# First sums of weight blocks: ScalarE and an adding DMA in place of a VectorE subtraction

## The chip, the cores and the metric

The kernel runs on one core of one Trainium2 chip. The metric is device time in microseconds (us) of one execution. The engines are named as the profile names them: PE (TensorE matmul), PEld (its weight load), DVE (VectorE), ACT (ScalarE), POOL (GpSimd), SP (SyncE, which issues the DMAs of the kernel before).

## What is computed

Two layers of a decoder over 512 tokens of 1024 features, all in float32. Layer 0 mixes tokens with gated linear attention (GLA), layer 1 with retention. Around each mixer stand two feed-forward blocks, so there are four of these; each ends in a layer norm.

```
def swiglu(x, w_in, w_out):
    gate, up = jnp.split(x @ w_in, 2, axis=-1)
    return (jax.nn.silu(gate) * up) @ w_out

def reference(x, ...):
    h = x
    for i in range(DEPTH):                      # DEPTH = 2
        h = layer_norm(DN_ALPHA * h + 0.5 * swiglu(h, ffn_w_in[i, 0], ffn_w_out[i, 0]), ...)
        m = gla_mixer(h, ...) if i == 0 else retention_mixer(h, ...)
        h = layer_norm(DN_ALPHA * h + m, ...)
        h = layer_norm(DN_ALPHA * h + 0.5 * swiglu(h, ffn_w_in[i, 1], ffn_w_out[i, 1]), ...)
    return h
```

`w_in` is 1024 x 5632 (gate and up of 2816 features), `w_out` 2816 x 1024.

## The kernel before

Weights come as granules of 1 MiB (128 partitions x 2048 float32), in the order in which they are used. `Stream` (lines 77 to 146) holds two load buffers `wf`: `load` (L92) has SP fetch granule i into one, and `prepare` (L108) makes from it the operands that PE takes. A float32 matrix product is done in three passes on operands that are split into hi + lo: `parts` (L101) casts a tile to hi on ACT (L105) and subtracts hi from it on DVE for lo (L106). `mm3` (L148) issues the three matmuls (L151 to L153). `next` (L137) returns granule i and prepares i + 1.

In a feed-forward block the hidden features come in 22 tiles of 128. For features 4 to 21 (`FAST`, 18 in each of the four blocks, 72 in all) gate and up are not taken as eight block products but as seven, `seven_products` (L323), by Winograd's form of Strassen's method over halves of tokens, input features and outputs. It needs sums of blocks of the weights, and these are what the change touches. With the granule's four blocks b11, b12, b22, b21 of 128 x 512, `prepare` forms the tile `t13` = [b12 - b11, b22 - b12] in one DVE subtraction over 1024 columns (L129), then `t24` = [b22 - t1, b21 - t2] in two over 512 (L130, L131), and splits both (`parts(st, t24)`, `parts(su, t13)`). Both tiles take the tag "sums", of which there are two buffers. The operands land in five buffers of 1024 columns and two of 512 (`slot`, L98), so a granule can be split only once PE is through with an earlier one.

The products of one such granule go to PSUM and are combined by DVE (L346, L348, L351, L353, L355) and ACT (L343, L349); the second product of a granule is written into the bank whose last content L351 reads. Between two such granules and the next two stands one granule of the output matrix (`out_steps`, L294), whose four results DVE adds to h (L275 or L277). So the order of use repeats itself: an odd feature X, an even feature Y, an output granule O, then X', Y', O'. A block has nine such pairs of X and Y, with the first pair partly at its start.

The order on each engine is not the order of the code: a scheduler of the framework sorts each engine's queue when the program is built, and puts semaphores where one engine reads what another wrote. Each queue is then worked through in order, so an instruction that waits holds up all behind it on its engine. POOL does nothing in the feed-forward blocks but L210, a power for the layer norm.

Names in the rows: `wf` a load buffer, `whi`/`wlo` the split weights, `sums` t13 or t24, `u`, `v`, `gate`, `up` and `products` those of `seven_products`, `sg`, `ahi`, `alo` the activation, `po` the output product.

Of the kernel before, what the change touches and what calls it, by code (L numbers as in the profile page):

```python
# [14 lines left out]
ALU = mybir.AluOpType  # L15
AX = mybir.AxisListType

P = 128
T = 512
NT = T // P  # L20
D = 1024
# [10 lines left out]
G = 2048  # L32
B = 512
GH, GDK, GDV, GRANK = 4, 128, 256, 16
RH, RDK, RDV = 4, 256, 512
CH = 64


def _ffn_plan():
    """The order of a feed-forward block's granules: ("in", f) for gate and up of  # L40
    128 features, ("out", c, i) for four units of the output product of chunk c,
    which lie between the features of the next chunk."""
    plan = []
    for c, (f0, f1) in enumerate(CHUNKS):
        n = 0
        for f in range(f0, f1):
            plan.append(("in", f))
            if c and (f - f0) % 2 == 0 and n < (CHUNKS[c - 1][1] - CHUNKS[c - 1][0]) // 2:
                plan.append(("out", c - 1, n))
                n += 1  # L50
    return plan + [("out", len(CHUNKS) - 1, i) for i in range((CHUNKS[-1][1] - CHUNKS[-1][0]) // 2)]


def _fast():
    """The granules of feed-forward weights that seven products take."""
    r, at = set(), 0
    plan = _ffn_plan()
    for mixer in (0, GH * 3 + GH, 0, RH * 6 + 2 * RH):
        at += mixer
        r |= {at + i for i, x in enumerate(plan) if x[0] == "in" and x[1] in FAST}  # L60
        at += len(plan)
    return r
# [3 lines left out]
def tile_decoder(ctx: ExitStack, tc: tile.TileContext, a: dict, out: bass.AP):  # L66
# [8 lines left out]

    # ---------------------------------------------------------------- weights
    class Stream:
        """The weights, 1 MiB at a time in the order of their use, each split
        exactly into two float32r parts."""

# [20 lines left out]
        def parts(self, slot, src, at=0):  # L101
            """src as hi + lo."""
            n = src.shape[-1]
            hi, lo = (x[:, at:at + n] for x in slot)
            nc.scalar.copy(hi, src)  # L105
            nc.vector.tensor_sub(lo, src, hi.bitcast(F32))  # L106

        def prepare(self, i):  # L108
# [3 lines left out]
            w = self.loaded[i]  # L112
            blk = lambda slot, c: tuple(x[:, c * B:(c + 1) * B] for x in slot)  # noqa: E731
            if i not in fast:
# [13 lines left out]
            t13, t24 = (self.sums_pool.tile([P, 2 * B], F32, tag="sums", name="sums", bufs=2) for _ in range(2))  # L128
            nc.vector.tensor_sub(t13, w[:, B:3 * B], w[:, :2 * B])  # L129
            nc.vector.tensor_sub(t24[:, :B], b22, t13[:, :B])  # L130
# [17 lines left out]
    def mm3(ps, l, r, start, stop):  # L148
        """One K tile of a float32 product: (hi + lo) x (hi + lo), with the three
        passes that reach float32's precision."""  # L150
        nc.tensor.matmul(ps, l[0], r[0], start=start, stop=False)  # L151
        nc.tensor.matmul(ps, l[0], r[1], start=False, stop=False)  # L152
        nc.tensor.matmul(ps, l[1], r[0], start=False, stop=stop)  # L153
# [3 lines left out]

    # ---------------------------------------------------------------- start
    hT = [None]
# [36 lines left out]

    # ---------------------------------------------------------------- layer norm
    def load_gb(tp, n, tags=("ln_g", "ln_b")):
# [7 lines left out]
    def rsqrt(tp, out_, in_, eps, n, scale=1.0):  # L206
        """(scale * (in_ + eps)) ** -0.5"""
        v = tp.tile([P, n], F32, tag="veps", name="veps", bufs=2)
        nc.vector.tensor_scalar(out=v, in0=in_, scalar1=eps, scalar2=scale, op0=ALU.add, op1=ALU.mult)
        nc.gpsimd.tensor_tensor(out=out_, in0=v, in1=mhalf[:, :n], op=ALU.pow)  # L210

    def layer_norm(tp, t, gb, last):
        """h[t] <- LN(h[t]); its transpose into hT."""
        x = h[t]
# [20 lines left out]

    # ---------------------------------------------------------------- products
    def feature_major(w, ranges, ps=None):
        """out[feature, token] of 2 tiles of 128 features."""
        w = [tuple(x.rearrange("p (k c) -> p k c", k=4) for x in b) for b in w]
        ps = ps or [pacc.tile([P, T], F32, tag="acc", name="fm") for _ in range(2)]  # L240
        for j in range(2):
            for r in ranges:
                for k in range(KD):
                    mm3(ps[j][:, r], pick(w[j if k < 4 else 3 - j], slice(None), k % 4),
                        pick(hT[0], slice(None), k, r), k == 0, k == KD - 1)
        return ps
# [6 lines left out]
    def two_granules_ahead():  # L253
        """The first two granules after a layer norm: the first half of the tokens
        is taken first, while the norm of the second half ends."""
        g = [ws.next(), ws.next()]
# [6 lines left out]
    def token_major(t, ws2, ps):  # L263
        """out[token, 512 columns] of one token tile."""
        for k in range(KD):
            mm3(ps, pick(hT[0], slice(None), k, slice(t * P, (t + 1) * P)), ws2[k // 4][k % 4], k == 0, k == KD - 1)
# [3 lines left out]
    def add_out(t, half, ps, first, tp=None):  # L270
        """h[t] <- alpha * h[t] + ps, or h[t] + ps; with tp, what the layer norm
        needs of it."""
        x = h[t][:, half * 512:(half + 1) * 512]
# [9 lines left out]
    class Units:  # L283
        """Units [P, 512] of the coming granules, four in each."""

# [8 lines left out]
    def out_steps(lhs, n, first, halves=(0, 1), tp=None):  # L294
        """h[:, half] += lhs^T @ W for all tokens, one K tile after the other: the
        steps, each to be given its unit."""
        for half in halves:
# [13 lines left out]
    def out_by_tokens(lhs, n, units, halves, first, tail=None, tp=None):  # L311
        """The same, one token tile after the other."""
        for t in range(NT):
# [7 lines left out]

    # ---------------------------------------------------------------- feed-forward
    def seven_products(w, s, tp):  # L323
        """gate and up [feature, token] of 128 features with the seven products of
        Winograd's form of Strassen's method, over halves of the tokens, of the
        features of h and of the outputs (gate and up)."""
        a11, a12, a22 = (pick(hT[0], slice(None), ks, ts)
# [12 lines left out]
        x, y, z, q = (bank(*b) for b in ((pacc, "acc"), (pacc, "acc"), (ptr, "tr"), (ptr, "tr")))  # L340
        # v = (p1, p1 + p6 + p7), u = (p1 + p6, p1 + p6 + p7)
        p1 = product(x[:, 0], a11, "b11")
# [15 lines left out]
    def operand_sums(tp):  # L358
        """The sums of blocks of h that seven_products takes, split."""
        s = [tuple(tp.tile([P, 4, H], F32R, tag=f"S{c}{i}", name=f"S{c}{i}", bufs=1) for c in ("hi", "lo")) for i in range(4)]  # L360
# [78 lines left out]

    # ---------------------------------------------------------------- mixers  # L440
    def gated_transpose(tp, y, n, gcol, bufs=1):
        """yT[n tiles of 128 features][tokens] * g, split."""
        res = []
# [12 lines left out]
    def gla(ln):  # L456
        with tc.tile_pool(name="gla", bufs=1) as tp:
# [22 lines left out]
            def gates(pg):  # L480
                """la[head] <- log sigmoid of the gates, [key feature, token]."""
                gl = tp.tile([2 * GRANK, T], F32, name="gl")
# [18 lines left out]
            def decays(hd):  # L501
                """exp of the gates' sums: within chunks of 64, and within blocks of 128
                from their start and to their end."""
                x64, x128 = (tp.tile([P, T], F32, tag=n, name=n) for n in ("x64", "x128"))
# [14 lines left out]
            def qk_of(ps, d):  # L519
# [3 lines left out]
                sc = float(GDK ** -0.5)  # L523
                v4 = lambda x: x.rearrange("p (n two c) -> p n two c", two=2, c=CH)  # noqa: E731
                nc.vector.scalar_tensor_tensor(out=w["qd"], in0=pq, scalar=sc, in1=d["e64"], op0=ALU.mult, op1=ALU.mult)
# [8 lines left out]
            def vr_of(g, between):  # L534
                """The values, and 2 silu(r); `between` is called before the last tokens."""
                v = tuple(tp.tile([P, NT, GDV], F32R, tag=f"v{c}", name=f"v{c}") for c in ("hi", "lo"))
# [208 lines left out]
def _weights(i):  # L745
    """All matrices as granules [P, G] in the order in which the kernel takes them."""
    def blocks(w):
        """[D, 256] as four blocks of [4 x 128, 128]: (0, 0), (0, 1), (1, 1), (1, 0)."""
        w = w.reshape(2, 4, P, 2, P).transpose(0, 3, 2, 1, 4)
# [46 lines left out]
def _constants():  # L796
    """Tables that depend on the shapes alone."""
    f = np.float32
# [34 lines left out]
```

## Time and profile before

| | |
|---|---|
| time, median of 3 runs (lowest to highest) | 2046.94 us (2045.32 to 2047.19) |
| the profiled execution: span from first to last instruction | 2044.7 us |
| PE busy | 2031.3 us, 99% |
| PEld busy | 1808.6 us, 88% |
| DVE busy | 1516.3 us, 74% |
| ACT busy | 796.8 us, 39% |
| POOL busy | 37.2 us, 2% |
| share of 16 DMA engines that the loads took | 28.2% |
| HBM read | 201.00 MB |

No time of the profiled execution is listed apart from its span. The span lies 0.6 to 2.5 us under the three runs, 2.2 us under their median. Shares are averages over stages: the feed-forward blocks and the mixers differ, and DVE is busier in the former. A busy share of PE counts modelled ends of pipelined matmuls, so what speaks for PE as the bound is that it hardly waits for anyone, not the 99% alone.

### The profile page before, as it was taken

What the parts mean: (1) busy time and instruction counts of PE and PEld (TensorE: products, weight loads), DVE (VectorE), ACT (ScalarE), POOL (GpSimd) and SP (SyncE); (2) the same over time, 40 slices, a digit from 0 to 9 for tenths busy, and PEclk for the clock granted to TensorE, in tenths of its full rate; (3) what the DMA queues carried; (4) which work ended last, traced back from release to release, by engine and by line L of the source; (5) the groups of instructions that cost most, each with busy time, mean ns of one, the idle gap of its engine ahead of it and who ended that gap; (6) DMA issues with size and microseconds to landing.
All of it is one profiled execution on the core that took longest, in us unless ns stands there. A gap on an engine that the chain in (4) does not pass through costs nothing.

```text
span 2044.7 us, 29592 instructions
## 1 busy us (share of the span) xinstructions
PE 2031.3 (99%) x12364; PEld 1808.6 (88%) x12364; DVE 1516.3 (74%) x2152; ACT 796.8 (39%) x1131; POOL 37.2 (2%) x56
## 2 busy tenths in 40 slices
PE   8999999999999999999999999999999999999998
PEld 7999998888889999998999998888888889999997
DVE  7888888745588888887888888554545468888886
ACT  5443433632234344343434443333232324443441
POOL 0000000000000000000000000000000000000000
PEclk9999999999999999999999999999999999999999
DMA  6322223112222222341322223222222222322322
GB/s 213 118 104 104 104 96 132 65 65 80 103 83 104 104 103 104 104 145 42 124 103 104 104 86 142 104 69 93 78 88 78 88 75 104 117 91 102 109 99 83
DMA packets 33637, 205.00 MB, mean 100 GB/s; under 512 B 5056, under 2 KB 5184, under 8 KB 10592
## 3 DMA queue, kind: packets, MB, share of 16 engines
q1 hardware_dynamic: 33504, 203.12, 28.2%
q8 instruction: 97, 1.59, 0.3%
q14 instruction: 36, 0.29, 0.0%
HBM read 201.00 MB, written 2.10 MB: 99 GB/s over the span
## 4 chain that ended last, share of the span: by engine, by line
PE 99%; DVE 0%; DMA 0%; ACT 0%; issue 0%; DVEq 0%
PE products L151 12%; PE products L152 12%; PE products L153 12%; PE po L151 10%; PE po L152 10%; PE po L153 10%; PE fm L152 5%; PE fm L151 5%; PE fm L153 5%; PE pvr L151 2%; PE pvr L152 1%; PE pvr L153 1%; PE pgg L151 1%; PE pgg L152 1%; PE pv L153 1%; PE pgg L153 1%
## 5 line engine op out<-in xcount | busy, mean ns | idle before, releaser
L106 DVE TENSOR_TENSOR wlo<-wf,whi 128x512 fp32r<-128x512 f32 (+1 forms) x362 | 399.6, 1108 | 97.6 <-ACT whi L105 97.2
L105 ACT CAST whi<-wf 128x512 fp32r<-128x512 f32 (+1 forms) x362 | 345.8, 958 | 300.6 <-PE po L153 130.6
L151 PE MATMUL products<-Shi,whi 128*128 128x256 f32 x1152 | 325.7, 283 | 0.0
L153 PE MATMUL products<-Shi,wlo 128*128 128x256 f32 x1152 | 325.6, 283 | 0.0
L152 PE MATMUL products<-Slo,whi 128*128 128x256 f32 x1152 | 325.6, 283 | 0.0
L151 PE MATMUL po<-whi,ahi 128*128 128x512 f32 x704 | 274.8, 391 | 0.0
L152 PE MATMUL po<-wlo,ahi 128*128 128x512 f32 x704 | 274.4, 390 | 0.0
L153 PE MATMUL po<-whi,alo 128*128 128x512 f32 x704 | 274.0, 389 | 0.0
L152 PE MATMUL products<-hTlo,whi 128*128 128x256 f32 x864 | 243.0, 281 | 0.0
L151 PE MATMUL products<-hThi,whi 128*128 128x256 f32 x864 | 242.9, 281 | 0.0
L153 PE MATMUL products<-hThi,wlo 128*128 128x256 f32 x864 | 242.0, 280 | 0.0
L153 PEld LDWEIGHTS products<-Shi,wlo 128*128 128x128 f32 x1152 | 220.4, 191 | 0.0
L151 PEld LDWEIGHTS products<-Shi,whi 128*128 128x128 f32 x1152 | 220.0, 191 | 0.3
L152 PEld LDWEIGHTS products<-Slo,whi 128*128 128x128 f32 x1152 | 220.2, 191 | 0.0
L105 ACT CAST whi<-sums 128x1024 fp32r<-128x1024 f32 x144 | 150.3, 1047 | 159.8 <-DVE h L277 87.7
L151 PE MATMUL fm<-hThi,whi 128*128 128x512 f32 (+1 forms) x592 | 202.9, 343 | 5.2 <-ACT hThi L183 5.2
L152 PE MATMUL fm<-hTlo,whi 128*128 128x512 f32 (+1 forms) x592 | 203.0, 343 | 0.0
L153 PE MATMUL fm<-hThi,wlo 128*128 128x512 f32 (+1 forms) x592 | 202.5, 342 | 0.0
L106 DVE TENSOR_TENSOR wlo<-sums,whi 128x1024 fp32r<-128x1024 f32 x144 | 175.7, 1222 | 24.0 <-ACT whi L105 24.0
L152 PEld LDWEIGHTS products<-hTlo,whi 128*128 128x128 f32 x864 | 163.0, 189 | 1.4
L151 PEld LDWEIGHTS products<-hThi,whi 128*128 128x128 f32 x864 | 162.9, 189 | 1.4
L153 PEld LDWEIGHTS products<-hThi,wlo 128*128 128x128 f32 x864 | 163.5, 189 | 0.0
(185 smaller groups left out, 3431.0 us busy)
## 6 DMA issues: line engine op xcount, KB each, us to landing
wf<-in_wts SPq DMA_DIRECT2D x179, 1024.0 KB, 4.8
ln_b<-in_ln_b SPq DMA_DIRECT2D x6, 512.0 KB, 3.7
ln_g<-in_ln_g SPq DMA_DIRECT2D x6, 512.0 KB, 5.2
xs<-in_xT SPq DMA_DIRECT2D x8, 256.0 KB, 5.3
h<-in_x SPq DMA_DIRECT2D x4, 512.0 KB, 7.8
out_h<-h SPq DMA_DIRECT2D x8, 256.0 KB, 2.0
wf<-in_wts SPq DMA_DIRECT2D x4, 256.0 KB, 5.8
dm<-in_decay SPq DMA_DIRECT2D x4, 256.0 KB, 3.2
```

The source lines that it names most:

```text
L105: nc.scalar.copy(hi, src)
L106: nc.vector.tensor_sub(lo, src, hi.bitcast(F32))
L151: nc.tensor.matmul(ps, l[0], r[0], start=start, stop=False)
L152: nc.tensor.matmul(ps, l[0], r[1], start=False, stop=False)
L153: nc.tensor.matmul(ps, l[1], r[0], start=False, stop=stop)
```

## The change

For each of the 72 granules that `seven_products` takes, `t13` is made in another way. ACT writes minus the first two blocks into the tile (`nc.scalar.mul(..., -1.0)`), and a DMA that POOL issues reads the second and third block again from DRAM and adds them to the tile (512 KB each). The weights are still loaded as a whole into `wf`. Everything else is the same; comments and docstrings were blanked, and all lines after 129 have a number that is larger by one (L130 is now the DMA, L131 and L132 the two subtractions of t24).

```
@@ Stream.prepare, a granule that seven_products takes @@
             self.parts(s11, b11)
             self.parts(sb, w[:, 2 * B:])
             t13, t24 = (self.sums_pool.tile([P, 2 * B], F32, tag="sums", name="sums", bufs=2) for _ in range(2))
-            nc.vector.tensor_sub(t13, w[:, B:3 * B], w[:, :2 * B])
+            nc.scalar.mul(t13, w[:, :2 * B], -1.0)
+            nc.gpsimd.dma_start(t13, wts[i, :, B:3 * B], accum_op=ALU.add)
             nc.vector.tensor_sub(t24[:, :B], b22, t13[:, :B])
             nc.vector.tensor_sub(t24[:, B:], b21, t24[:, :B])
             self.parts(st, t24)
             self.parts(su, t13)
```

PE and SP have the same instructions in the same order as before. Here is DVE's queue around an even feature Y, first before (wf10 is Y's load buffer, sums_1004 its t13, sums_1005 its t24, sums_925 the t13 of X):

```order
L394 SCALAR_TENSOR_TENSOR sg_906<-sg_906,up_808 128x512
L106 TENSOR_TENSOR wlo_993<-wf10_934,whi_992 128x512
L129 TENSOR_TENSOR sums_1004<-wf10_934 128x1024
L398 TENSOR_TENSOR alo_910<-sg_906,ahi_909 128x512
L130 TENSOR_TENSOR sums_1005<-wf10_934,sums_1004 128x512
L131 TENSOR_TENSOR sums_1005<-wf10_934,sums_1005 128x512
L106 TENSOR_TENSOR wlo_995<-wf10_934,whi_994 128x1024
L275 SCALAR_TENSOR_TENSOR h0_67<-h0_67,po_936 128x512
```

Now (Y's t13 is sums_1008, its t24 sums_1009):

```order
L395 SCALAR_TENSOR_TENSOR sg_909<-sg_909,up_811 128x512
L106 TENSOR_TENSOR wlo_997<-wf10_938,whi_996 128x512
L399 TENSOR_TENSOR alo_913<-sg_909,ahi_912 128x512
L131 TENSOR_TENSOR sums_1009<-wf10_938,sums_1008 128x512
L132 TENSOR_TENSOR sums_1009<-wf10_938,sums_1009 128x512
L106 TENSOR_TENSOR wlo_999<-wf10_938,whi_998 128x1024
L276 SCALAR_TENSOR_TENSOR h0_67<-h0_67,po_940 128x512
```

L129 has gone. The first subtraction of t24 (L130, now L131) stands in the same place, right behind `alo`, and now waits for the DMA instead of for DVE's own subtraction; behind it stand the other subtraction, lo of Y's blocks, and the additions to h.

ACT's queue over the same stretch, before (sums_926 is the t24 of X, wf12 the load buffer of X'):

```order
L105 CAST whi_917<-sums_926 128x1024
L105 CAST whi_992<-wf10_934 128x512
L105 CAST whi_919<-sums_925 128x1024
L397 CAST ahi_909<-sg_906 128x512
L105 CAST whi_994<-wf10_934 128x1024
L105 CAST whi_996<-sums_1005 128x1024
L343 COPY v_1018<-products_1019 128x256
L105 CAST whi_1237<-wf12_1129 128x512
L349 COPY v_1018<-u_1017 128x256
L105 CAST whi_998<-sums_1004 128x1024
```

Now (the t24 of X is sums_929, its t13 sums_928; sums_1254 is the t13 of X'):

```order
L105 CAST whi_920<-sums_929 128x1024
L105 CAST whi_996<-wf10_938 128x512
L105 CAST whi_922<-sums_928 128x1024
L129 ACTIVATE sums_1008<-wf10_938 128x1024
L398 CAST ahi_912<-sg_909 128x512
L105 CAST whi_998<-wf10_938 128x1024
L105 CAST whi_1000<-sums_1009 128x1024
L344 COPY v_1023<-products_1024 128x256
L105 CAST whi_1242<-wf12_1134 128x512
L129 ACTIVATE sums_1254<-wf12_1134 128x1024
L350 COPY v_1023<-u_1022 128x256
L105 CAST whi_1002<-sums_1008 128x1024
```

The negation of Y stands behind the cast of X's t13. It waits for DVE's last read of X's t24 (sums_929), whose buffer it writes. The negation of X' stands behind the cast of its first block and ahead of the copy to `v`, and waits for DVE's last read of Y's t24 (sums_1009).

## Rows read from the trace of the kernel before

**Rows 1.** The page: span, and busy time of each engine

```profile
span 2044.7 us, 29592 instructions
...
PE 2031.3 (99%) x12364; PEld 1808.6 (88%) x12364; DVE 1516.3 (74%) x2152; ACT 796.8 (39%) x1131; POOL 37.2 (2%) x56
```

**Rows 2.** Waits of PE, longest first: waiter, releaser, us in total, times, longest

```profile
PE fm L151 <- ACT hThi L183: 5.2, 1, 5.2
PE po L151 <- ACT yhi L450: 0.3, 1, 0.3
```

**Rows 3.** Busy time by window, one period of a pair of granules

```profile
core 0: us, PE busy (x) PEld busy (x) DVE busy (x) ACT busy (x) POOL busy (x), PEclk, DMA share, GB/s
647.97:678.88 30.91, 30.91 (x218) 29.02 (x218) 25.47 (x35) 13.04 (x19) 0.00 (x0) 1.00 0.30 102
```

**Rows 4.** Groups by line: count, busy us, mean ns of one, idle before

```profile
L105 ACT CAST whi<-sums 128x1024 fp32r<-128x1024 f32 x144 | 150.3, 1047 | 159.8 <-DVE h L277 87.7 <-DVE h L275 35.1 <-PE po L153 17.5
...
L129 DVE TENSOR_TENSOR sums<-wf 128x1024 f32<-128x1024 f32 x72 | 87.9, 1221 | 1.0
...
L210 POOL TENSOR_TENSOR lnr<-veps,mhalf 128x1 f32<-128x1 f32 x24 | 22.1, 921 | 1469.2 <-DVE veps L209 1469.2
...
L210 POOL TENSOR_TENSOR rr<-veps,mhalf 128x1 f32<-128x1 f32 x16 | 8.7, 548 | 353.2 <-ACT yhi L450 266.0 <-DVE yt L710 72.0 <-DVE veps L209 15.2
```

**Rows 5.** Timeline of DVE, one pair: start, length, instruction, idle before

```profile
665.46 1.22 DVE L106 TENSOR_TENSOR wlo<-sums,whi 128x1024 fp32r<-128x1024 f32 x1
...
669.26 1.22 DVE L129 TENSOR_TENSOR sums<-wf 128x1024 f32<-128x1024 f32 x1
670.40 0.69 DVE L398 TENSOR_TENSOR alo<-sg,ahi 128x512 fp32r<-128x512 f32 x1
671.00 0.69 DVE L130 TENSOR_TENSOR sums<-wf,sums 128x512 f32<-128x512 f32 x1
...
672.33 1.22 DVE L106 TENSOR_TENSOR wlo<-wf,whi 128x1024 fp32r<-128x1024 f32 x1
674.50 2.73 DVE L275 SCALAR_TENSOR_TENSOR h<-h,po 128x512 f32<-128x512 f32 x4 [0.94 <-PE po L153]
677.62 1.23 DVE L106 TENSOR_TENSOR wlo<-sums,whi 128x1024 fp32r<-128x1024 f32 x1 [0.40 <-ACT whi L105]
...
680.81 0.42 DVE L346 TENSOR_TENSOR u<-v,products 128x256 f32<-128x256 f32 x1
...
683.74 0.69 DVE L351 TENSOR_TENSOR gate<-v,products 128x512 f32<-128x512 f32 x1 [1.06 <-PE products L153]
...
689.63 0.69 DVE L130 TENSOR_TENSOR sums<-wf,sums 128x512 f32<-128x512 f32 x1
```

**Rows 6.** Timeline of ACT, around the same pair and at a block's first pair

```profile
626.40 0.63 ACT L105 CAST whi<-wf 128x512 fp32r<-128x512 f32 x1
...
657.10 0.37 ACT L343 COPY v<-products 128x256 f32<-128x256 f32 x1 [0.54 <-PE products L153]
...
678.38 0.63 ACT L105 CAST whi<-wf 128x512 fp32r<-128x512 f32 x1
682.71 0.41 ACT L349 COPY v<-u 128x256 f32<-128x256 f32 x1 [3.70 <-DVE u L348]
```

**Rows 7.** Timeline of SP, weight loads

```profile
664.97 0.33 SPq L92 DMA_DIRECT2D wf<-in_wts  x1
...
673.58 0.33 SPq L92 DMA_DIRECT2D wf<-in_wts  x1
```

**Rows 8.** DMA issues: destination<-source, queue, count, KB each, us to landing

```profile
wf<-in_wts SPq DMA_DIRECT2D x179, 1024.0 KB, 4.8
ln_b<-in_ln_b SPq DMA_DIRECT2D x6, 512.0 KB, 3.7
...
h<-in_x SPq DMA_DIRECT2D x4, 512.0 KB, 7.8
out_h<-h SPq DMA_DIRECT2D x8, 256.0 KB, 2.0
```

More of the change, by code (lines that the diff above doesn't have):

```diff
@@ L128, in prepare @@
             t13, t24 = (self.sums_pool.tile([P, 2 * B], F32, tag="sums", name="sums", bufs=2) for _ in range(2))
-            nc.vector.tensor_sub(t13, w[:, B:3 * B], w[:, :2 * B])
+            nc.scalar.mul(t13, w[:, :2 * B], -1.0)
+            nc.gpsimd.dma_start(t13, wts[i, :, B:3 * B], accum_op=ALU.add)
             nc.vector.tensor_sub(t24[:, :B], b22, t13[:, :B])
```

## The prediction

> **What bounds the kernel now.** I read the waits of PE first. PE waits twice in the whole trace, 5.2 us for its first operand and 0.3 us near a layer norm [rows 2]. So PE's own matmuls set the end: of the span of 2044.7 us it is busy for 2031.3 [rows 1]. The table by window then shows how a feed-forward block runs: one period, a pair of granules X and Y and an output granule O, takes 30.91 us, PE is busy for all of it at full clock, DVE for 25.47 and ACT for 13.04 [rows 3]. DVE has 5.4 us of slack in each period, and nothing of it reaches the end. What DVE and ACT save is worth nothing by itself; the question is only whether the new wait grows until PE runs dry. For that I went through the timeline of DVE, ACT and SP around one Y (rows 5 to 7).
>
> **What goes and what comes.** L129 goes: 72 subtractions at 1.22 us, 87.9 us of DVE [rows 4], all of it beside PE's work, so the span changes by 0. ACT gets 72 negations of 128x1024. A cast of that shape takes 1.05 us there [rows 4], so 75 us, 2.1 in a period that has 17.9 us of ACT idle: 0. POOL gets 72 DMA issues, on a queue that is empty in these blocks. The DMA engines get 72 times 512 KB from DRAM, and as much read from and written to the tile.
>
> The cost that matters is D, the time from the end of the negation to the landing of the added blocks. The trace has no adding DMA and none that POOL issues. From below: a 256 KB store lands after 2.0 us [rows 8]; adding can't land sooner than a plain move of half its bytes. From above: 512 KB that had to share the queue with other loads landed after 7.8 us [rows 8], and POOL needs 0.92 us for its smallest instruction [rows 4], which gives 8.7. A plain 512 KB lands in 3.7 us, and 1 MB in 4.8 [rows 8]. An adding DMA has 1 MB to read (512 KB in DRAM, 512 KB in the tile), so the 1 MB row is the nearest; with 0.92 for POOL I take D = 5.7 us.
>
> The Trainium skill ("Collectives: The Full Stack", on the bandwidth ceiling and the fold count) says that adding under way is slow through the second operand's reads, not through the adder. No run here shows it; by it, too, the 1 MB row would be the right one. A reader may leave this out; D above is from rows.
>
> **Where D is met.** There are two kinds of granule.
>
> Y. Its negation writes the buffer of X's t24, which DVE last reads in L106 from 665.46 to 666.68 [rows 5]. So the negation ends at 667.73, and the landed tile is there at 667.7 + D. DVE, without L129, would come to L130 at 669.9 (671.00 less 1.14, the step from 669.26 to 670.40). So D over 2.1 us stops DVE, with D = 5.7 for 3.6 us, until 673.4. Queued behind it are the second half of t24, the lo of Y's blocks, four additions to h, the lo of t24, and then the combinations of the next products.
>
> X'. Its negation needs X's load buffer filled. That load leaves SP when DVE is through with the lo of Y's blocks: lo from 672.33 to 673.55, load issued at 673.58 [rows 5, 7]. The load takes 4.8 us [rows 8], and ACT casts the first block at 678.38 [rows 6]. Its L130 stands at 689.63 [rows 5], so D is hidden there as long as little else is late.
>
> **The loop.** Each wait delays the next negation, so I add one period up, in steps of DVE as the rows give them (1.14 for a 1024-column step, 0.6 for 512, 0.72 where the next one reads the last, 0.33 for 256). From L130 of Y: the lo of Y's blocks ends at 2.55 (0.72 + 0.61 + 1.22); load 4.8, to 7.35; cast 0.63, to 8.0; negation 1.05, to 9.05; then D, and L130 of X' at 9.1 + D. DVE itself needs about 15.4 us of work and cast to get there (8.0 to the cast, 0.6 for its lo, 1.8 to the start of L351, 5.0 for the six steps after it), so D up to 6.3 costs nothing here. From L130 of X' to the end of the lo of its t24: 7.2 us (1.94 for L130, L131 and L398; 0.33 and 0.42 for L346 and L348; 0.41 for the copy to `v` [rows 6]; the cast of X's blocks on ACT, 1.05, and of its t24, after the 0.63 of the activation; 1.22 for the lo). Then Y's negation, 1.05, and D again. The loop takes 17.35 + 2D, or 23.7 + D where D is under 6.3. It fits into 30.91 us up to D = 6.8.
>
> First pair of a block. X's first block is cast by 627.03 [rows 6], its negation ends at 628.1, L130 comes at 628.1 + D. Through t24 and its lo (4.85 us) and Y's negation, Y's L130 comes at 634.0 + 2D, and 10.5 us later L351 (2.55, 4.8, 0.63, then lo 0.6, and 1.9 through L346, L348, copy and L351) has emptied a bank that PE writes from 657.1, when the first product of the next granule is done [rows 6]. This fits up to D = 6.3.
>
> **Sum.** D = 5.7 is under both. DVE stops for some 3.6 us in each of 36 Y, about 130 us in all, in its own 5.4 us of slack plus the 1.2 twice that L129 leaves; PE stops for 0. The profiled span stays at 2044.7 and the time where the median of before is, 2.2 us above it: 2047 us. The margin is thin, 1.1 us of D in the loop and 0.6 at the start.
>
> The Trainium skill ("DMA: Bandwidth & Descriptors", rules for kernel authors) advises to issue a DMA early and wait for it late. The trace of before has just that for the weight loads; the change does it for X and not for Y, where one instruction lies between [order of DVE above]. By this rule alone Y is where time would be lost; rows give DVE's slack, which the rule doesn't weigh.
>
> **Rivals.** (1) The add lands late, and DVE's wait becomes PE's. For it: D is on no row, and adding two streams may be slower than moving one of twice the size; against: the sum above. It decides from D = 6.3 on. Four block starts cost 2 us for each us over it, and 32 periods (nine pairs less the first, in four blocks) 2 us for each us over 6.8, so 64 us in all for each us. At D = 7.5: 10 + 45, 2102 us. At the upper bound of 8.7: 19 + 122, 2188 us; at twice 5.7, 41 + 294, 2382.
> (2) DVE holds POOL up. The power on POOL takes 0.92 us in one place and 0.55 in another [rows 4], so something beside it matters. If POOL can build the DMA only in DVE's gaps, Y's waits until DVE stops at L130, 2.1 us after the negation, and X's for at most a step of 1.14. The two D add up to 14.6, 1.1 over the 13.6 that the loop bears: 32 x 1.1 = 35 us, and 2.0 over the 12.6 of a block's start, four times, 8 us: 2090 us. Against it: DVE stops by itself just there. The Trainium skill ("SBUF — State Buffer", who interferes with whom) says that DVE instructions with two SBUF inputs contend with GpSimd's reads, but infers that building descriptors is spared. No trace here shows either.
> (3) Faster. 87.9 us of DVE are free, and PE waits in places. But PE's waits are 5.5 us, all at the start and at a layer norm [rows 2], and the change lies in neither; with 2 to 4 us gained at the tail of a block it would be 2042 us. The rows speak against it: PE is 30.91 of 30.91 us busy [rows 3].
>
> **How the numbers follow.** Forecast, hidden in DVE's slack: 0.48, own range 2043 to 2051. Rival 1: 0.37. Rival 2: 0.10. Rival 3: 0.05. A change of 0.2% (4 us) is about what a measurement of this kernel can tell from none: the three runs differ by 0.1%. Slower by more than that are rivals 1 and 2, 0.47; faster 0.05; the same 0.48. The range reaches from rival 3 to the time at the upper bound of D, 2042 to 2190; beyond it lies only an add of over 8.7 us, which I give 0.13, and 0.02 below.
>
> **What the new profile would show.** If right: PE's waits as before, 5 to 6 us; a period still 30.9 us; DVE idle ahead of the first t24 subtraction, put down to the DMA into `sums`, some 36 times and about 3.6 us each; those DMAs landing after 5 to 6.3 us; DVE's 25.5 us in a period down to 23.0. If rival 1: PE waits ahead of `products` for DVE or ACT, periods longer than 31 us, and landings of over 6.8 us. If rival 2: a short landing but POOL late in issuing. Wrong altogether would be PE waits in a period while the adds land within 6 us, or an add landing near 6 us with DVE not waiting for it at all.

## The result, and the profile after

The changed kernel takes 2076.11 us (median of 4 runs, 2074.79 to 2077.26), the kernel before 2046.81 beside it (2045.32 to 2047.19). The ratio is 1.0142 (95% interval 1.0128 to 1.0156), so 29.3 us were lost; the forecast's own range was 2043 to 2051. The page of the profile after, against [rows 1], and its DMA issue against [rows 8]:

```profile
span 2073.9 us, 29738 instructions
...
PE 2039.4 (98%) x12364; PEld 1813.4 (87%) x12364; DVE 1424.5 (69%) x2080; ACT 869.2 (42%) x1203; POOL 100.6 (5%) x128
...
sums<-in_wts POOLq DMA_DIRECT2D x72, 512.0 KB, 5.4
```

The span grew by 29.2 us. DVE is 91.8 us less busy, ACT 72.4 more and POOL 63.4 more. PE, with the same 12364 matmuls, is 8.1 us busier, so the other 21.1 us are idle time of PE. The waits of PE, against [rows 2], and behind them the one new wait among DVE's (us in total, times, longest):

```profile
PE products L152 <- ACT v L344: 14.8, 4, 5.2
PE fm L152 <- ACT hThi L184: 5.5, 1, 5.5
PE products L152 <- DVE u L349: 4.4, 6, 1.4
PE po L152 <- ACT yhi L451: 0.3, 1, 0.3
...
DVE sums L131 <- DMA sums<-in_wts: 133.5, 37, 7.1
```

`v` on L344 is ACT's copy of a granule's first product out of PSUM, `u` on L349 the sum into which DVE takes the fourth. DVE's wait for the add is there 37 times, 133.5 us, and yet PE lost only 19.2 us in new waits. They come in four long ones, one at each block's start, and six short ones, one of them (1.06 us) right behind the long one of the first block. Most periods are unharmed. The windows of the changed kernel (us, then busy time and instructions of PE, PEld, DVE, ACT, POOL, granted clock, DMA share, GB/s) show one period, against [rows 3], and then the second block's start:

```profile
100.75:131.66 30.91, 30.91 (x218) 29.02 (x217) 22.87 (x34) 15.02 (x20) 1.73 (x3) 1.00 0.51 137
...
654.00:658.60 4.60, 0.98 (x9) 0.78 (x7) 3.84 (x6) 1.32 (x2) 0.00 (x0) 0.96 0.17 27
658.60:662.00 3.40, 3.35 (x17) 3.35 (x18) 2.11 (x3) 0.00 (x0) 0.00 (x0) 0.55 0.67 277
662.00:665.00 3.00, 3.00 (x27) 2.96 (x26) 1.69 (x4) 2.27 (x4) 0.87 (x1) 1.00 0.00 0
```

The period has no idle PE at full clock. At the block's start PE works for 0.98 of 4.6 us, and the granted clock of the 3.4 us behind that is 0.55, near the lower of its two levels (1.2 of 2.4 GHz), before it is back at 1.00. Behind the long pauses of the third and fourth block (3.18 and 5.17 us) the clock was 0.50 for 5.7 us and 0.56 for 3.6 us; behind that of the first (2.81 us) it stayed at 1.00. The slow stretches cost 1.5, 2.9 and 1.6 us, about 6 of the 8.1 us of added PE time.

One ordinary Y of the changed kernel in the timeline (start, duration, engine, line; in brackets the idle time ahead and its releaser), against [rows 5, 6]:

```profile
99.39 1.06 ACT L129 ACTIVATE sums<-wf 128x1024 f32<-128x1024 f32 x1
...
100.75 0.86 POOL L130 DMA_DIRECT2D sums<-in_wts  x1 [15.12 <-ACT sums L129]
...
106.14 0.69 DVE L131 TENSOR_TENSOR sums<-wf,sums 128x512 f32<-128x512 f32 x1 [3.34 <-DMA sums<-in_wts]
```

The negation ends at 100.45 and the sum is taken up at 106.14: D is 5.69 us. POOL issues 0.30 us behind the negation, though DVE is busy just then; so it is in 68 of the 72, and 0.97 us is the longest.

The second block's start, where PE paused (engines in turn: ACT, POOL, SP, DVE, PE; X is feature 5, Y feature 6):

```profile
633.48 1.06 ACT L129 ACTIVATE sums<-wf 128x1024 f32<-128x1024 f32 x1
648.03 1.06 ACT L129 ACTIVATE sums<-wf 128x1024 f32<-128x1024 f32 x1 [0.43 <-DVE wlo L106]
657.28 1.04 ACT L105 CAST whi<-sums 128x1024 fp32r<-128x1024 f32 x1 [5.60 <-DVE sums L132]
658.23 0.37 ACT L344 COPY v<-products 128x256 f32<-128x256 f32 x1
662.08 0.62 ACT L105 CAST whi<-wf 128x512 fp32r<-128x512 f32 x1 [3.49 <-DMA wf<-in_wts]
...
634.85 0.87 POOL L130 DMA_DIRECT2D sums<-in_wts  x1 [20.45 <-DVE wlo L106]
649.39 0.88 POOL L130 DMA_DIRECT2D sums<-in_wts  x1 [13.68 <-ACT sums L129]
...
634.90 0.33 SPq L92 DMA_DIRECT2D wf<-in_wts  x1
657.25 0.33 SPq L92 DMA_DIRECT2D wf<-in_wts  x1
...
643.24 0.69 DVE L131 TENSOR_TENSOR sums<-wf,sums 128x512 f32<-128x512 f32 x1 [5.83 <-DMA sums<-in_wts]
654.76 0.69 DVE L131 TENSOR_TENSOR sums<-wf,sums 128x512 f32<-128x512 f32 x1 [3.31 <-DMA sums<-in_wts]
655.37 1.22 DVE L106 TENSOR_TENSOR wlo<-wf,whi 128x1024 fp32r<-128x1024 f32 x1
656.51 0.68 DVE L132 TENSOR_TENSOR sums<-wf,sums 128x512 f32<-128x512 f32 x1
663.86 0.42 DVE L349 TENSOR_TENSOR u<-u,products 128x256 f32<-128x256 f32 x1
...
658.65 0.58 PE L152 MATMUL products<-Shi,whi 128*128 128x256 f32 x1 [3.67 <-ACT v L344]
```

Two adds run one after the other here. The first is issued at 634.85, in the same moment as a weight load of 1 MB (634.90), and DVE takes it up at 643.24, 8.4 us later, where 5.4 is the usual landing. In the four blocks this first add, that of feature 5, takes 7.7, 8.4, 6.9 and 9.7 us from issue to L131. Only then comes X's t24 and with it Y's negation (648.03), and Y's add is taken up at 654.76, after 5.67 us from the end of its negation. ACT casts Y's t24 at 657.28, and behind that cast, in ACT's queue, stands the copy to `v` (658.23) that PE waits for. One thing more is new here. In the kernel before, lo of Y's blocks (L106) stands behind both subtractions of t24. In the changed kernel the scheduler has put it between them in three of the four block starts, which holds up the end of t24, and with it the cast and the copy, by 1.0 us.

### The profile page after: what moved, and what is told of

Same layout as the page of the kernel before. It is cut to its first block, busy times and chain, and to the rows that moved or that the text cites. A ratio compares the mean times of both kernels' runs of the same rounds, so it can differ in the third digit from the quotient of the medians.

```text
span 2073.9 us, 29738 instructions
## 1 busy us (share of the span) xinstructions
PE 2039.4 (98%) x12364; PEld 1813.4 (87%) x12364; DVE 1424.5 (69%) x2080; ACT 869.2 (42%) x1203; POOL 100.6 (5%) x128
## 4 chain that ended last, share of the span: by engine, by line
PE 72%; issue 19%; DVE 5%; DMA 2%; POOL 1%; ACT 1%; SPq 0%; DVEq 0%; POOLq 0%; ACTq 0%
PE po L152 7%; PE po L154 7%; PE po L153 7%; PE products L152 7%; PE products L153 7%; PE products L154 7%; PE fm L154 3%; PE fm L153 3%; PE fm L152 3%; PE pvr L152 1%; PE pvr L154 1%; PE pvr L153 1%; PE pgg L152 1%; PE pv L152 1%; PE pgg L154 1%
## 5 line engine op out<-in xcount | busy, mean ns | idle before, releaser
L106 DVE TENSOR_TENSOR wlo<-wf,whi 128x512 fp32r<-128x512 f32 (+1 forms) x362 | 399.7, 1108 | 156.2 <-ACT whi L105 155.9
L152 PE MATMUL products<-Shi,whi 128*128 128x256 f32 x1152 | 329.7, 286 | 19.4 <-ACT v L344 14.8
L106 DVE TENSOR_TENSOR wlo<-sums,whi 128x1024 fp32r<-128x1024 f32 x144 | 175.2, 1219 | 12.1 <-ACT whi L105 12.1
```

## The experiments

The theories that the expectations name: A, the loss lies in the four block starts, through two adds in a row; B, in every period, through DVE's wait; C, in ACT's negations (in the last experiment C is a price of each add). All times are medians; the kernel before took 2046.4 to 2046.9 us beside them. The scheduler orders each version anew: the plain move, the exchanged products and the free bank keep the order of the changed kernel on every queue, in the others some instructions of ACT and DVE move.

**Where: the first pair alone, and all but the first.**

```
e2_first_pair_dma: the changed form for features 5 and 6 of a block only
+            if nth[i] not in (1, 2):          # place among a block's 18 granules, from 0
+                nc.vector.tensor_sub(t13, w[:, B:3 * B], w[:, :2 * B])
+            else: (negation and adding DMA)
e1_first_x_dve: the changed form for all but feature 5
+            if nth[i] == 1:  (VectorE's subtraction)
```

> The reverse: only the first pair of each block (features 5 and 6, 8 granules in all) is made by negation and adding DMA, the other 64 by DVE's subtraction. Theory A: the four pauses stay, without the short waits for u later in the blocks: 2065 to 2073 us. Theory B: 8 of 72 adds, 2048 to 2051 us. Theory C: 2050 us.

> Only the second fast granule of each of the four blocks (feature 5, the X of the first pair) gets its first sums from DVE's subtraction again; the other 68 keep the negation and the adding DMA. Theory A (the loss is made at the four block starts: two adds in a row, the first of them slowed by a weight load, hold ACT's copy to v and so PE, and the clock falls after each pause): the four pauses of 2.8 to 5.2 us and their slow clock go, some 22 of the 29 us; what stays is the short waits for u, so 2047 to 2055 us. Theory B (the loss is made in every period, by DVE's 3.4 us wait there): 4 of 72 adds less, 2072 to 2076 us. Theory C (ACT's 72 negations hold PE): 2074 us.

The first pair alone took 2071.68 us, ratio 1.0123 (1.0108 to 1.0138): 8 of 72 granules make 25 of the 29 us. All but feature 5 took 2053.12, ratio 1.0033 (1.0021 to 1.0044). The waits of PE in the one and in the other:

```profile
PE products L156 <- ACT v L348: 15.3, 4, 4.7
```

```profile
PE products L156 <- DVE u L353: 3.9, 7, 1.2
```

The four long waits come with the first pair and go with the add of feature 5. B falls. What remains without feature 5 is a handful of short waits for `u`.

**ACT's negations.**

```
e7_negate_only: the addition by VectorE, no DMA
-            nc.gpsimd.dma_start(t13, wts[i, :, B:3 * B], accum_op=ALU.add)
+            nc.vector.tensor_add(t13, t13, w[:, B:3 * B])
```

> ACT's negation as in the changed kernel, but DVE adds the other blocks from the load buffer; no adding DMA. Theories A and B (the landing time of the DMA is the cause): DVE's work is that of before and ACT's 75 us lie beside PE's work, 2045 to 2049 us. Theory C (ACT's negations, which stand ahead of its copies to v, hold PE): 2060 us or more.

2046.67 us, ratio 1.0000 (0.9990 to 1.0009). The 72 negations cost nothing; C falls.

**Only the second add of the pair taken out.**

```
e10_first_y_dve: as e1, but for feature 6
+            if nth[i] == 2:  (VectorE's subtraction)
```

> Only the even feature of the first pair of each block (feature 6) gets its sums from VectorE's subtraction again; the other 68 granules keep the negation and the adding DMA, the slowed add of feature 5 among them. Theory A (PE is held by the sum of two adds in a row: in the second block 8.7 + 5.7 us from end of negation to landing, 14.4, where about 10.5 fits): without the second the chain is 4 to 5 us shorter than it needs, so no waits of PE for v at the block starts and 2047 to 2054 us. Rival A2 (the one add that shares the DMA engines with a weight load is enough to hold PE): the waits for v stay, 2065 to 2075 us.

2059.78 us, ratio 1.0065 (1.0050 to 1.0080): between the two, and a miss for both. PE's waits:

```profile
PE products L156 <- DVE u L353: 4.3, 6, 1.1
PE products L156 <- ACT v L348: 4.0, 3, 2.2
```

The waits for `v` fell from 14.8 to 4.0 us, but one slowed add is already too much. So the first pair has less room than I had taken it to have.

**The load beside the first add.**

```
e12_small_load: for feature 6, whose load leaves with the add of feature 5 (M = 128)
-                    nc.sync.dma_start(self.loaded[i], wts[i])
+                    nc.sync.dma_start(self.loaded[i][:, :M], wts[i, :, :M])
(feature 6 takes all its blocks from these 128 columns, broadcast)
```

> The weight load that is issued together with the add of feature 5 (that of feature 6, once in each of the four blocks) brings 64 KB in place of 1 MB; feature 6 takes its blocks from these 128 columns, read again and again, so its results are left out; every instruction and add stays. Theory A-load (that load is what makes the first add land after 7 to 9.7 us): the first adds land within 5.8 us, PE waits for v 0.5 to 1.2 us at each start in place of 2.8 to 5.2, 2051 to 2060 us. Rival A-first (the first adds of a block are late by themselves, by their place or a queue that was empty): landings stay at 7 to 9.7 us, 2072 to 2078 us.

2062.43 us, ratio 1.0079 (1.0062 to 1.0096), a little over the range given. Landing of all adds, PE's waits, and the second block's start on PE:

```profile
DMA to landing us min/median/max: 5.2/5.4/6.9
...
PE products L176 <- DVE u L373: 6.0, 8, 1.1
PE products L176 <- ACT v L368: 4.2, 4, 1.3
...
653.21 0.39 PE L176 MATMUL products<-Shi,whi 128*128 128x256 f32 x1 [1.33 <-ACT v L368]
658.78 0.39 PE L176 MATMUL products<-Shi,whi 128*128 128x256 f32 x1 [1.03 <-DVE u L373]
```

The four adds of feature 5 land after 5.5 to 5.7 us now (6.9 to 9.6 in the changed kernel), and the waits for `v` fall from 14.8 to 4.2. The load that leaves beside the add does slow it, and the time is 13.8 of the 29.3 us better. That is about what the load costs, not exactly: the order at the block starts is another one here (at the second, the way from the first add to Y's negation is 1.3 us longer and that from the second add to the end of the copy 1.0 shorter). The other 15.5 us are lost though both adds land as the prediction had it.

**Adding or moving.**

```
e4_plain_move: the same bytes without the addition (the sum is left out)
-            nc.gpsimd.dma_start(t13, wts[i, :, B:3 * B], accum_op=ALU.add)
+            nc.gpsimd.dma_start(t13, wts[i, :, B:3 * B])
```

> POOL's DMA moves the 512 KB and doesn't add them (the sum is left out, the tile holds the two blocks). Theory A-add (the 5.4 us are those of reading and writing the tile beside the DRAM read): it lands after 3.5 to 4.5 us, PE waits 0 to 1.5 us at each start, 2047 to 2058 us, and DVE's waits fall from 133 to about 85 us. Rival A-issue (POOL's way of issuing costs the time): landing stays at 5 to 5.5 us, 2072 to 2078 us.

2055.07 us, ratio 1.0039 (1.0024 to 1.0054). Landing and PE's waits:

```profile
sums<-in_wts POOLq DMA_DIRECT2D x72, 512.0 KB, 3.9
...
PE products L152 <- DVE u L349: 4.3, 4, 1.6
PE products L152 <- ACT v L344: 1.2, 2, 0.7
```

A plain 512 KB from POOL's queue lands after 3.9 us, near the 3.7 of one from SP [rows 8]; adding makes it 5.4. So the 1.5 us come with the addition, not with POOL's queue as such; 0.3 of them are POOL's own, which is busy for 0.87 us at an adding issue and for 0.54 at a plain one. The Trainium skill ("Collectives: The Full Stack", on the bandwidth ceiling and the fold count) puts such a price, for the adds of a collective, to the second operand's reads; the run shows the price, not which part of the transfer it is.

**The bank that PE waits for.** A bank of PSUM holds two of these products, and PE's waits show that it writes one half only when the reader of the other is through. First the third and fourth product are exchanged in all 72 granules; then three products of feature 5 move, so that PE comes to the bank that ScalarE's copy reads with its sixth product and no longer with its third.

```
e6_other_bank
-        p6 = product(x[:, 1], s[1], "t2")
+        p6 = product(y[:, 0], s[1], "t2")
-        p7 = product(y[:, 0], s[2], "t3")
+        p7 = product(x[:, 1], s[2], "t3")
e14_free_bank: feature 5 only (first is n == 5)
+        at6, at7, at5 = (y[:, 0], q[:, 1], x[:, 1]) if first else (x[:, 1], y[:, 0], y[:, 1])
(the third, fourth and sixth product are written to at6, at7 and at5)
```

> The changed kernel, with the third and fourth product of a granule exchanged between the two PSUM banks: the third (t2) goes beside the sixth, the fourth (t3) beside the first. So the fourth product, 1.4 us later, is the first that PE may not write before ACT has copied the first one out to v, and the sixth product waits for the first u and no longer for the second. Theory A, with ACT's copy behind the cast of t24 as what PE waits for: each of the four pauses is shorter by up to 1.4 us and the six waits for u (4.4 us in all) go: 2062 to 2070 us. Rival (PE waits for t24's split itself, and the copy is only the last of several): the third product waits for its operand instead, 2074 to 2077 us.

> Only in the first odd feature of each block (feature 5) the products go to other banks: the third to the half of bank y, the fourth to the free half of q, the sixth to the free half of x. So PE does not write into the bank that ScalarE's copy to v reads until three products later. The order on every engine and all sums are as in the changed kernel. Theory A (the nearer deadline is ScalarE's queue: the cast of Y's second sums, late by the two adds, stands ahead of the copy, and PE needs the bank behind the copy): PE's 14.8 us of waits for v go or shrink to under 4 us, some of it comes back behind it, since VectorE is still late by the 1.8 us a start that my own deadline gave: 2050 to 2062 us. Rival B (PE would be held as long anyway, by operands or by VectorE): other waits of 2.5 to 5 us take their place at the four starts, 2068 to 2077 us.

The exchange took 2067.49 us, ratio 1.0099 (1.0082 to 1.0116), as theory A had it, but the waits for `u` did not go: they are 6.4 us now, for L347. The free bank took 2075.18, ratio 1.0139 (1.0122 to 1.0156): no gain, rival B. PE's waits in the first, then in the second, and where it stopped there at the second block's start:

```profile
PE products L152 <- ACT v L344: 7.6, 4, 2.8
PE products L152 <- DVE u L347: 6.4, 5, 2.0
...
PE products L152 <- DVE u L349: 17.4, 7, 3.9
...
664.96 0.47 PE L152 MATMUL products<-Shi,whi 128*128 128x256 f32 x1 [3.79 <-DVE u L349]
```

PE passes the copy and stops four products later, ahead of its seventh, for nearly as long (3.79 against 3.67), behind L349. My theory that the copy alone decides falls. Behind Y's late t24 hang two chains that come out within a few us of each other: cast and copy on ACT; and the load of X' (657.25) into the buffer whose last reader is Y's t24, cast (662.08), lo and L349 on DVE. To free one shows the other.

**Four buffers for the sums.**

```
e3_four_sums
-NFC = 10
+NFC = 8
-            t13, t24 = (... tag="sums", name="sums", bufs=2) for _ in range(2))
+            t13, t24 = (... tag="sums", name="sums", bufs=4) for _ in range(2))
```

> Four buffers for the sums in place of two (paid for with 8 in place of 10 buffers for the split activations). The negation of Y no longer waits until DVE has read X's second sums. Theory A: the two adds of a first pair need not run one after the other, Y's is landed before DVE asks for it, PE's waits for v at the block starts go, and DVE's waits for the adds fall from 133 to under 60 us: 2047 to 2056 us. Rival (the pair is held by something else, or the fewer activation buffers hold it): 2065 us or more.

2171.00 us, ratio 1.0604 (1.0589 to 1.0620), against every theory. The scheduler, with other buffers to wait for, wrote another order: X's first subtraction of t24 now stands ahead of `gate` instead of behind `sg`. DVE in a steady period:

```profile
192.62 0.69 DVE L131 TENSOR_TENSOR sums<-wf,sums 128x512 f32<-128x512 f32 x1 [5.20 <-DMA sums<-in_wts]
193.23 0.68 DVE L352 TENSOR_TENSOR gate<-v,products 128x512 f32<-128x512 f32 x1
```

X's add was hidden by the place of L131 in DVE's queue; ahead of `gate` the same add holds up what PE waits for, in each period. So the run doesn't test what it was made for. It shows that the cover of a wait is one row of the order.

**A longer D.**

```
e5_add_twice: D doubled (the sums are others)
             nc.gpsimd.dma_start(t13, wts[i, :, B:3 * B], accum_op=ALU.add)
+            nc.gpsimd.dma_start(t13, wts[i, :, B:3 * B], accum_op=ALU.add)
```

> The same 512 KB are added a second time by a second DMA behind the first (so the sums are others), which makes the way from negation to landed tile about twice as long, 10.5 to 11.5 us. The loop sum of the prediction (17.35 + 2D, in 30.91 us) then decides: at D = 11.2 a period takes 39.8 us, 8.8 more, in 32 periods 283 us, and about 40 us at the block starts: 2330 to 2400 us, with PE waiting in every period. Rival (the loop is more elastic than that sum, and only block starts cost): 2110 to 2180 us.

2456.49 us, ratio 1.2005 (1.1987 to 1.2023), over the range given. PE's waits, a period by DVE's first subtraction of t24 (Y, X', Y'), POOL's and SP's issues for X', and the granted clock of the period:

```profile
PE products L153 <- DVE u L350: 324.7, 36, 12.2
...
171.49 0.69 DVE L132 TENSOR_TENSOR sums<-wf,sums 128x512 f32<-128x512 f32 x1 [6.70 <-DMA sums<-in_wts]
197.73 0.69 DVE L132 TENSOR_TENSOR sums<-wf,sums 128x512 f32<-128x512 f32 x1 [5.92 <-DMA sums<-in_wts]
214.57 0.69 DVE L132 TENSOR_TENSOR sums<-wf,sums 128x512 f32<-128x512 f32 x1 [7.06 <-DMA sums<-in_wts]
...
183.76 0.86 POOL L130 DMA_DIRECT2D sums<-in_wts  x1 [16.75 <-ACT v L345]
192.36 0.86 POOL L131 DMA_DIRECT2D sums<-in_wts  x1 [7.73 <-DMA sums<-in_wts]
...
183.79 0.33 SPq L92 DMA_DIRECT2D wf<-in_wts  x1
...
171.49:214.57 43.08, 33.74 (x216) 31.64 (x216) 23.47 (x33) 14.68 (x20) 3.46 (x4) 0.86 0.50 122
```

The first add of X' leaves in the same moment as a weight load again (183.76 and 183.79), and the second is issued 8.6 us behind it, so D is 14.3 us for X' (negation's end at 183.47 to 197.73) and 11.65 for Y' (202.92 to 214.57). The loop sum then gives 17.35 + 14.3 + 11.65 = 43.3 us; the period is 43.08. What I missed was, once more, a load beside the add. But only the total of the sum holds. From Y's L132 to the end of the negation of X' it had 9.05 us, and here it is 12.0, since in this version's order that negation stands behind two more of ACT's casts; from L132 of X' to the end of the negation of Y' it had 8.25, and here it is 5.2. The two errors cancel, which is luck.

**Only where the wait is hidden.**

```
e15_odd_only: the changed form for the odd features behind a block's first pair
+            if nth[i] % 2 == 0 or nth[i] == 1:  (VectorE's subtraction)
```

> The negation and the adding DMA only for the 32 odd features behind the first pair of each block, where the prediction said that the add is hidden by 9 us of other work of VectorE; the 40 others (all even features, and feature 5) by VectorE's subtraction. Theory A (time is lost only where VectorE reaches the wait before the add has landed and PE runs out behind it, which is never so here): PE waits 5 to 6 us in all, the adds land within 7 us, VectorE's busy time falls by about 39 us against before, and the time is that of before, 2044 to 2049 us. Rival C (some of the loss is a price of each add, by the DMA engines or the loads they slow): with 32 of 72 adds 12 of the 29 us, 2055 to 2062 us.

2046.17 us, ratio 0.9999 (0.9990 to 1.0009). The page, and DVE's saving against [rows 1]:

```profile
span 2044.2 us, 29652 instructions
...
PE 2030.0 (99%) x12364; PEld 1806.6 (88%) x12364; DVE 1480.2 (72%) x2120; ACT 828.3 (41%) x1163; POOL 66.0 (3%) x88
```

32 adds cost nothing, and DVE's 36 us less buy nothing. The advice of the Trainium skill that the prediction cites ("DMA: Bandwidth & Descriptors", rules for kernel authors: issue early, wait late) agrees here: the adds that are waited for late are free. No version here beats the kernel before.

## Why the prediction went wrong, step by step

The forecast was no change, 2047 us. What came is rival 1's kind (DVE's wait becomes PE's), at 2076 us, but only in one of the two places that rival 1 priced.

- **D**: 5.7 us forecast, 5.69 in an ordinary Y. Right, and its two terms nearly so: 0.92 for POOL and 4.8 for the transfer forecast; 0.30 until POOL starts, 0.86 to 0.88 for POOL at nearly every issue and 4.5 behind that seen.
- **DVE's waits**: 36 of about 3.6 us, 130 in all, at each Y forecast; 37 and 133.5 us seen. Of these 32 are at a Y (112 us, 3.5 each), and four, 21 us in all, at feature 5, where none was forecast; that the totals agree is in part luck. In steady state they are hidden in DVE's slack as the prediction said (30.91 of 30.91 us of PE).
- **The loop sum**, 17.35 + 2D: the total fits a period of 43.08 us with doubled adds (43.3), its pieces don't; in the changed kernel itself nothing tests it, since the loop isn't what limits a period there.
- **ACT's negations and DVE's freed time worth nothing**: right (2046.67 and 2046.17 us).
- **Rival 2, DVE holding POOL up**: POOL issues 0.30 us behind the negation while DVE works. Wrong, as was thought likely.
- **"First pair of a block ... This fits up to D = 6.3"**: this step failed, in both its parts.

The first part is the limit. The chain to Y's L131, at 634.0 + 2D, was right: with the measured 8.70 (634.54 to 643.24) and 5.67 us it gives 648.4, and the trace has 648.2 (654.76 less the 6.56 us by which this kernel was late before it came there, read from one copy of `v`: 632.69 now, 626.13 before). But I took as the deadline the bank that L351 (L352 now) reads, 10.5 us behind and needed at 657.1. PE needs two others sooner. In the trace of before, its third and its sixth product of feature 5 begin here:

```profile
648.26 0.28 PE L151 MATMUL products<-Shi,whi 128*128 128x256 f32 x1
...
652.55 0.28 PE L151 MATMUL products<-Shi,whi 128*128 128x256 f32 x1
```

The third writes the bank that the copy to `v` reads, and the copy ends 3.84 us behind the start of L131 (654.76 to 658.60, by ACT's queue, which the prediction did not follow here; 1.0 of it is the L106 that the new order puts ahead of L132). The sixth writes the bank that L349 reads, which ends 9.52 us behind L131 (to 664.28). So 634.0 + 2D + 3.84 must not be over 648.26, and 634.0 + 2D + 9.52 not over 652.55: D up to 5.2 by the first, and up to 4.5 by the second, in place of 6.3. Even with D = 5.7 a start then costs 2.4 us; where no load slowed the add, the two D at this start were 5.99 and 5.71 us, which by the same sum costs 2.7 (the order was another one), and PE waited 1.33 + 1.03 = 2.36. The first limit leaves 10.4 us for the two D of a start. They came to 13.7, 14.4, 13.0 and 15.9 us in the four blocks, so PE should wait 3.3, 4.0, 2.5 and 5.4; it waited 2.8, 3.7, 3.2 and 5.2.

The second part is a term that was missing: one D was put in for both adds, but that of feature 5 leaves together with a weight load and takes up to 9.7 us. At the second block the two come to 14.4, 5.4 over the 9.0 that fit. PE waited 3.67 us, and lost 1.5 more in the 3.4 us at a clock of 0.55: 5.2. The first wait, with the slow work behind it, is long enough here that the second chain is not seen, which is why the free bank gained nothing: there the sixth product is free, and the seventh, 1.43 us later, waits for L349. The two D were 14.6 us there, 5.6 over; less 1.4 that is 4.2, and 3.79 was measured.

Where the 29 us went: about half (13.8 us) to the load beside the first add, most of the rest to two adds of 5.7 us in 9.0, and a few us to short waits inside blocks, probably where an add or a load lands later than usual (with feature 5 alone left as before, the other adds cost 6.7 us over the kernel before, 2053.12 against 2046.38). The slow clock after three of the pauses, about 6 us, is contained in these. Rival 1's other part, 32 periods, cost nearly nothing, since D stayed at 5.7 there.

Open: why the first add took 6.9 us in one block and 9.7 in another, beside the same kind of load (the load had left 1.62 us ahead of the add where it took 6.9, 1.30 ahead at 7.7, and in the same moment at 8.4 and 9.7), and which of a few late adds and loads made each of the short waits.

## What to carry to other kernels

Where a wait is added, walk through every queue behind it, on each engine that takes up the late tile, and set each arrival against the first instruction of the bounding engine that needs it: the nearest deadline decides, not the one that is seen first, and several may lie within a microsecond of each other. Price a transfer with what is issued in the same moment, and do it apart for the start of a stage, where two late steps stand in a row. Work moved off an engine that has slack earned nothing here, and it cost where the new wait was met early.

## What the runs showed of the hardware that was not expected

- An add of 512 KB into SBUF lands after 5.4 us (median), a plain move of the same bytes from POOL's queue after 3.9; POOL is busy 0.87 us for the one and 0.54 for the other.
- With a 1 MB load that left in the same moment or up to 1.6 us earlier an add of the changed kernel landed after 6.9 to 9.6 us (four times); with one that left 3.1 us earlier, after 5.1 to 6.9; with none within 6 us, after 5.2 to 6.2, and once 7.3.
- After a pause of 3.67 us PE's granted clock was 0.55 for 3.4 us, after one of 2.81 us it stayed at 1.00. With a pause of 9.1 us in each period the clock of a whole period was 0.86, and PE's busy time 79 us longer (2110.7 against 2031.3).
